# Turned tiles of the MLP's hidden layer: four places of halves, two places for the last tile, and steps begun one pair sooner

## The chip, the cores and the metric

The kernel runs on one core of a Trainium2 chip. The metric is the device time of one execution in microseconds (us). TensorE is called PE, VectorE DVE, ScalarE ACT, GpSimd POOL, and SyncE, which issues most of the DMAs, SP.

## The reference

One layer on 256 rows of 2048 features, in float32: a norm, a mixer of an SSD scan and attention (not touched here), its product with w_out, and then an MLP with the square of a relu:

```python
h = h + rmsnorm(mix, norm_mix_post)
hdn = relu(rmsnorm(h, norm_mlp_pre) @ w_up)      # 256 x 8192
h = h + rmsnorm((hdn * hdn) @ w_down, norm_mlp_post)
```

The change is in the MLP. The 8192 hidden features are made in two halves of 4096, each with its part of w_up and then its part of w_down.

## The kernel before, in words

**Products.** A float32 product is made of three matmuls in a reduced format: each operand is split into a high half `hi` (made by ACT, line 148) and the rest `lo` (made by DVE, line 149), and high x high, high x low and low x high are added up. The weights come as raw blocks of 128 x 2 x 512 (512 KB) through `fetch` (line 162, on SP), and are then split. Where a Strassen-like scheme replaces eight block products by seven (`seven`, lines 423 to 457), DVE also makes sums of blocks (line 263), and one raw block comes in two DMAs (lines 157 and 158), half of it a sum that POOL's DMAs made in memory.

**Units.** `unit` (line 488) makes 2 x 512 columns for both tiles of 128 rows: a list of pairs of row tiles of the contraction, some by seven products and the others as plain row tiles (`row_tiles`, lines 368 to 370). For w_up the pairs are 0 to 6, of which 1, 3, 4 and 6 go by seven, and pair 7 as plain row tiles at the end. After the last pair by seven, `combine_new` (lines 459 to 468) puts the four sums of products together: ACT copies one (line 464), and DVE adds (lines 465 to 468) into four tiles, `room["shared"]`: two in hb and two called wpost. Line 468 is the last and writes `b[1]`, the second wpost tile. After that, pair 7 ends in the other four banks, `up_end` adds them to the tiles (line 1491), and the two sets of four banks change roles. So the next unit's first row tiles want the banks that the combine reads.

**Turned tiles.** Each of a unit's four finished tiles (128 rows x 512 hidden features) has to be turned, since w_down contracts over the features. `turned` does this in two steps, beside the next unit's products:

- first step, begun by `pump_beside`: ACT takes the relu (line 1500) and the square (line 1501), and writes the tile's words as separate 16-bit halves (line 1502) into a place of `room["halves"]`; a transposing DMA on SP (line 1503) turns the halves back into the tile's own memory.
- second step, run by `land_beside` or `drain_beside`: ACT puts the halves together to words again (line 1506) in a tile called junk, of which there is one, and ACT and DVE split it (lines 148 and 149) into sh and sl or ah and al, where w_down reads them.

There are two places of halves (for four tiles). A unit begins the first step of one tile before each of its pairs from the third on (`if i >= 2`), and the second step after more than two further pairs. What is left after the last pair by seven is finished by `drain_beside` ahead of the combine. The order of instructions on each engine is set by a scheduler from priorities; an engine runs its instructions in that order.

**Places of raw weights.** Besides four places of its own pool, the raw weights use memory that is free at the time: in w_up's first half two parts of mw0, all of mw2 and three parts of ha (10 places in all, while mw1 holds the halves); in the second half two parts of ha (6 in all), while the first part of ha holds the halves. The last w_down begins with two parts of uc and what the halves left of ha, and adds the place of the halves (`more_in_place`) once all tiles are turned.

Of the kernel before, what the change touches and what calls it, by code (L numbers as in the profile page):

```python
# [17 lines left out]
P = 128  # L18
# [60 lines left out]
def hymba_layer(ctx: ExitStack, tc: tile.TileContext, x, norm_mix_pre, w_in, conv_w, conv_b, dt_bias, a_log,  # L79
# [113 lines left out]
    def beside_up(raws, turn, halves=None):  # L193

        room["sums"] = [v[:, k:k + KB] for k in range(0, NK // 2, KB) for v in att[1]]
        b = hp.tile([P, NT, NB], F32, name="hb")
        room["shared"] = [[b[:, t] for t in range(NT)],
                          [hp.tile([P, NB], F32, name="wpost", bufs=2) for _ in range(NT)]]
        a = hp.tile([P, 3 * KB, NB], F32, name="ha")
        in_a = [a[:, k:k + KB] for k in range(0, 3 * KB, KB)]  # L200
        halves = in_a.pop(0) if halves is None else halves
        room["halves"] = deque(halves[:, i].bitcast(U16) for i in range(KB))
        room["raw"], room["turn"], room["acts"], room["chain"] = [*raws, *in_a], turn, act_u, True
        room["of_halves"], room["of_a"] = halves, in_a
        sums_of.clear()

    def beside_down():

        a = hp.tile([P, 3 * KB, 2, S], F32R, name="ha")
        room["sums"] = [a[:, k] for k in range(3 * KB)]  # L210
        room["raw"], room["turn"], room["acts"], room["then"] = [mws[2]], 0, part, more_beside_down
        sums_of.clear()

    def more_beside_down():
# [273 lines left out]
    def unit(src, n, order, last, acc, more, combine, lag=0, at_end=(None, None), first=True, ending=None,  # L488
# [3 lines left out]
        cols = blocks_of(n)  # L492
        sevens = [k for k, by_seven in order if by_seven]
        for i, (k, by_seven) in enumerate(order):
            if i >= 2:
                pump_beside()
            if i + 1 < len(order) and order[i + 1][1]:
                sums_of_acts(order[i + 1][0])
            if by_seven:
                if k == sevens[0]:  # L500
                    drain()
                    if ready:
                        ready()
                seven(src, *cols, k, acc, more, k == sevens[0], k == sevens[-1])
            else:
                for b in range(2):
                    row_tiles(src, cols[b], [k], acc[b::2], room["acts"], first and i == 0, False,
                              fetch=fetch_next)
            land_beside()
            if k == sevens[-1]:  # L510
                drain_beside()
                combine(more)
        for b in range(2):
            if b and ending:
# [960 lines left out]
    def out_of_place():  # L1475

        yield from copies(in_dram, of_h, 4)
        beside_up([*tiles_of(mws[0], (0, NB)), mws[2]], -2 * RAWS, mws[1])
        for k in UP_SEVENS:
            sums_of_acts(k)  # L1480
            yield
# [13 lines left out]
    def turned(t, k, r):  # L1495
# [6 lines left out]
        nc.scalar.activation(halves.rearrange("p (h n) -> p h n", h=2), words.rearrange("p (n h) -> p h n", h=2), AF.Copy)  # L1502
        nc.sync.dma_start_transpose(words.rearrange("p (n s) -> p n s", s=P), halves)
        yield
        whole = hp.tile([P, NB], F32, name="junk")
        nc.scalar.activation(whole.bitcast(U16).rearrange("p (n h) -> p h n", h=2), words.rearrange("p (h n) -> p h n", h=2), AF.Copy)  # L1506
        d_h, d_l, i = part(k)
        split(d_h[:, i:i + 4, ts], d_l[:, i:i + 4, ts], whole.rearrange("p (f s) -> p f s", f=4))

    def onto_new_mw(more):  # L1510

# [14 lines left out]
    for hf in range(2):  # L1526
        if hf:
            beside_up([], 0)
        for fb in range(0 if hf else 2, 8, 2):
            unit(w_ups[hf], fb, orders[("up", hf), fb], (7,), acc, more,  # L1530
                 lambda x: combine_new(room["shared"], x), 0, (up_end(fb, 0), up_end(fb + 1, 1)))
            acc, more = more, acc
# [24 lines left out]
    def more_in_place():  # L1557
# [1 line left out]
        b = hp.tile([P, KB, 2, S], F32R, name="hb")  # L1559
        room["sums"] += [b[:, k] for k in range(KB)]  # L1560
        room["turn"] %= RAWS + len(room["raw"])
        room["raw"].append(room["of_halves"])
        for n in range(2):
            load_wpost(norm_mlp_post, n)

    room["then"] = more_in_place
    unit(w_downs[1], 0, orders[("down", 1), 0], (14, 15), acc, more,
         lambda x: combine_onto(0, x), 0, (complete(0), complete(1)))
    room["chain"] = False
# [36 lines left out]
```

## Time and profile before

| | |
|---|---|
| median of 3 runs | 1448.58 us (1446.73 to 1452.11) |
| the profiled execution | 1448.34 us |
| its span, first to last instruction | 1446.6 us |
| PE, DVE, ACT busy | 99%, 90%, 69% of the span |
| mean DMA rate | 235 GB/s |
| L1506, junk<-hb and junk<-wpost | 14 + 14 operations, median 1.37 us each |

A row of the profile names the source line, engine, operation, and tiles as out<-in, with shapes as partitions x elements. In the timeline the first number is the start from the beginning of the span, the second the duration; a bracket gives the idle time of the engine just before, and what ended it. A wait for several semaphores is put down to the one that came last. A line can be that of a helper: all high halves are on L148, all low halves on L149. The w_up units of the second half run from about 1110 to 1273 us, and the last w_down follows.

### The profile page before, as it was taken

What the parts mean: (1) busy time and instruction counts of PE and PEld (TensorE: products, weight loads), DVE (VectorE), ACT (ScalarE), POOL (GpSimd) and SP (SyncE); (2) the same over time, 40 slices, a digit from 0 to 9 for tenths busy, and PEclk for the clock granted to TensorE, in tenths of its full rate; (3) what the DMA queues carried; (4) which work ended last, traced back from release to release, by engine and by line L of the source; (5) the groups of instructions that cost most, each with busy time, mean ns of one, the idle gap of its engine ahead of it and who ended that gap; (6) DMA issues with size and microseconds to landing.
All of it is one profiled execution on the core that took longest, in us unless ns stands there. A gap on an engine that the chain in (4) does not pass through costs nothing. (4 is left out here: it accounts for less than half of the span.)

```text
span 1446.6 us, 20277 instructions
## 1 busy us (share of the span) xinstructions
PE 1432.3 (99%) x6930; PEld 1201.5 (83%) x6930; DVE 1297.6 (90%) x1881; ACT 1000.4 (69%) x1407; POOL 162.6 (11%) x244
## 2 busy tenths in 40 slices
PE   9999999999999999999999999999999999999998
PEld 8888888888888888888888888878888878877886
DVE  7788888988999778689988999999889989989998
ACT  7577669666666666556667668986565689987664
POOL 0201110131111000011100011011111111111000
PEclk9999999999999999999999999999999999999999
DMA  8977656756888648588976799798888999999864
GB/s 268 273 217 225 190 175 186 236 175 195 232 245 255 192 126 251 168 268 261 275 235 213 203 340 288 197 266 244 257 254 262 253 268 288 247 280 293 264 197 150
DMA packets 201927, 340.31 MB, mean 235 GB/s; under 512 B 45616, under 2 KB 48544, under 8 KB 201824
## 3 DMA queue, kind: packets, MB, share of 16 engines
q1 hardware_dynamic: 174304, 279.72, 62.0%
q0 software_dynamic: 19648, 45.63, 15.5%
q10 hardware_dynamic: 7872, 13.68, 2.8%
q8 instruction: 54, 0.88, 0.3%
q14 instruction: 49, 0.40, 0.1%
HBM read 327.39 MB, written 49.84 MB: 261 GB/s over the span
## 5 line engine op out<-in xcount | busy, mean ns | idle before, releaser
L149 DVE TENSOR_TENSOR lo<-raw,hi 128x1024 fp32r<-128x1024 f32 (+1 forms) x390 | 472.6, 1217 | 82.8 <-ACT hi L148 80.6
L148 ACT ACTIVATE hi<-raw 128x1024 fp32r<-128x1024 f32 (+1 forms) x390 | 406.2, 1048 | 170.2 <-PE acc L370 49.1
L526 PE MATMUL acc<-ua,hi 128*128 128x512 f32 x520 | 141.2, 400 | 0.1
L148 ACT ACTIVATE hi<-e 128x1024 fp32r<-128x1024 f32 x66 | 69.7, 1057 | 53.8 <-DVE e L263 50.2
L526 PEld LDWEIGHTS acc<-ua,hi 128*128 128x128 f32 x520 | 91.2, 189 | 14.2 <-ACT hi L148 0.2
L368 PE MATMUL acc<-hi,ua 128*128 128x512 f32 x228 | 90.4, 396 | 0.4 <-DVE wpost L468 0.4
L368 PE MATMUL acc<-hi,sh 128*128 128x512 f32 x220 | 86.6, 394 | 3.0 <-DVE wpost L468 3.0
L369 PE MATMUL acc<-lo,ua 128*128 128x512 f32 x228 | 89.2, 391 | 0.0
L370 PE MATMUL acc<-hi,ua 128*128 128x512 f32 x228 | 89.1, 391 | 0.0
L149 DVE TENSOR_TENSOR lo<-e,hi 128x1024 fp32r<-128x1024 f32 x66 | 80.4, 1218 | 6.4 <-ACT hi L148 6.2
L370 PE MATMUL acc<-hi,sl 128*128 128x512 f32 x220 | 85.7, 390 | 0.0
L369 PE MATMUL acc<-lo,sh 128*128 128x512 f32 x220 | 85.6, 389 | 0.0
L529 PEld LDWEIGHTS acc<-ua,lo 128*128 128x128 f32 x520 | 76.5, 189 | 8.9
L529 PE MATMUL acc<-ua,lo 128*128 128x256 f32 x520 | 78.8, 281 | 0.0
L456 PE MATMUL acc<-lo,ah 128*128 128x512 f32 x180 | 70.6, 392 | 0.7 <-DVE lo L149 0.7
L457 PE MATMUL acc<-hi,al 128*128 128x512 f32 x180 | 70.1, 389 | 0.0
L455 PE MATMUL acc<-hi,ah 128*128 128x512 f32 x180 | 70.1, 389 | 0.0
L526 PE MATMUL acc<-uc,hi 128*128 128x512 f32 x208 | 61.4, 405 | 0.0
L149 DVE TENSOR_TENSOR lo<-ha,hi 128x1024 fp32r<-128x1024 f32 x48 | 58.3, 1218 | 3.0 <-ACT hi L148 2.7
L148 ACT ACTIVATE hi<-ha 128x1024 fp32r<-128x1024 f32 x48 | 50.2, 1050 | 6.9 <-PE acc L370 2.0
L456 PE MATMUL acc<-lo,ua 128*128 128x512 f32 x137 | 53.4, 390 | 0.2 <-DVE lo L149 0.2
L455 PE MATMUL acc<-hi,ua 128*128 128x512 f32 x137 | 53.5, 391 | 0.0
(565 smaller groups left out, 3717.0 us busy)
## 6 DMA issues: line engine op xcount, KB each, us to landing
raw<-in_w_in_dram SPq DMA_DIRECT2D x154, 512.0 KB, 4.4
raw<-in_w_down_dram SPq DMA_DIRECT2D x70, 512.0 KB, 5.7
raw<-in_w_up_dram SPq DMA_DIRECT2D x65, 512.0 KB, 5.0
raw<-in_w_out_dram SPq DMA_DIRECT2D x38, 512.0 KB, 5.2
raw<-pair SPq DMA_DIRECT2D x59, 256.0 KB, 4.7
pair<-in_w_up_dram POOLq DMA_DIRECT2D x56, 256.0 KB, 5.8
pair<-in_w_down_dram POOLq DMA_DIRECT2D x52, 256.0 KB, 5.9
ha<-in_w_up_dram SPq DMA_DIRECT2D x25, 512.0 KB, 6.8
```

The lines of the kernel that those rows point to most:

```text
L148: return (nc.scalar.activation(hi, src, AF.Copy), nc.vector.tensor_tensor(lo, src, hi.bitcast(F32), op=ALU.subtract))
L149: nc.vector.tensor_tensor(lo, src, hi.bitcast(F32), op=ALU.subtract))
L368: nc.tensor.matmul(dst[:, cs], a_h[:, r, ts], hi[:, j, cs], start=begin and j == 0, stop=False)
L369: nc.tensor.matmul(dst[:, cs], a_h[:, r, ts], lo[:, j, cs], start=False, stop=False)
L370: product[t] = nc.tensor.matmul(dst[:, cs], a_l[:, r, ts], hi[:, j, cs], start=False, stop=end and j == KB - 1)
L455: nc.tensor.matmul(dst, a_h, hi[:, j], start=own and first, stop=False)
L456: nc.tensor.matmul(dst, a_h, lo[:, j], start=False, stop=False)
L457: nc.tensor.matmul(dst, a_l, hi[:, j], start=False, stop=own and last)
L526: nc.tensor.matmul(acc[f], hi[:, j, f * P:(f + 1) * P], u(k0 + j), start=k0 + j == 0, stop=False, skip_group_check=True)
L529: nc.tensor.matmul(acc[f][:, 0], lo[:, j, f * P:(f + 1) * P], u(k0 + j)[:, 0], start=False, stop=k0 + j == NK - 1, skip_group_check=True)
```

## The change

- `turned` puts the words together in the tile's own place of halves, not in junk, and splits from there.
- There are four places of halves in place of two: mw1 and one part of mw0 in w_up's first half, two of the three parts of ha in its second. The raw weights have 9 places instead of 10 in the first half, 5 instead of 6 in the second. The last w_down begins with one place fewer, and gets two instead of one when all tiles are turned.
- `b[1]`, the tile turned last, has two places in turn: the wpost tile and the memory of junk.
- In w_up the first steps begin at the unit's second pair (`room["first"]` is 1), in w_down at the third as before. `drain_beside` isn't called in a unit any more: at this pace the last second step follows the last pair by seven.

```diff
@@ beside_up
+        room["last"] = deque([room["shared"][1].pop(), hp.tile([P, NB], F32, name="junk")])
+        room["shared"][1].append(room["last"][0])
         a = hp.tile([P, 3 * KB, NB], F32, name="ha")
         in_a = [a[:, k:k + KB] for k in range(0, 3 * KB, KB)]
-        halves = in_a.pop(0) if halves is None else halves
-        room["halves"] = deque(halves[:, i].bitcast(U16) for i in range(KB))
+        halves = halves or [in_a.pop(0) for _ in range(2)]
+        room["halves"] = deque(v[:, i].bitcast(U16) for v in halves for i in range(KB))
         room["raw"], room["turn"], room["acts"], room["chain"] = [*raws, *in_a], turn, act_u, True
-        room["of_halves"], room["of_a"] = halves, in_a
+        room["of_halves"], room["of_a"], room["first"] = halves, in_a, 1
...
@@ unit
-            if i >= 2:
+            if i >= room.get("first", 0):
                 pump_beside()
...
             land_beside()
             if k == sevens[-1]:
-                drain_beside()
                 combine(more)
...
@@ out_of_place
-        beside_up([*tiles_of(mws[0], (0, NB)), mws[2]], -2 * RAWS, mws[1])
+        some, more_raw = tiles_of(mws[0], (0, NB))
+        beside_up([more_raw, mws[2]], -2 * RAWS, [mws[1], some])
...
@@ turned
-        whole = hp.tile([P, NB], F32, name="junk")
-        nc.scalar.activation(whole.bitcast(U16).rearrange("p (n h) -> p h n", h=2), words.rearrange("p (h n) -> p h n", h=2), AF.Copy)
+        nc.scalar.activation(halves.rearrange("p (n h) -> p h n", h=2), words.rearrange("p (h n) -> p h n", h=2), AF.Copy)
         d_h, d_l, i = part(k)
-        split(d_h[:, i:i + 4, ts], d_l[:, i:i + 4, ts], whole.rearrange("p (f s) -> p f s", f=4))
+        split(d_h[:, i:i + 4, ts], d_l[:, i:i + 4, ts], halves.bitcast(F32).rearrange("p (f s) -> p f s", f=4))
...
@@ the loop over w_up's units
         for fb in range(0 if hf else 2, 8, 2):
+            room["last"].rotate(1)
+            room["shared"][1][1] = room["last"][0]
             unit(w_ups[hf], fb, orders[("up", hf), fb], (7,), acc, more,
...
@@ the last w_down
-        room["raw"].append(room["of_halves"])
+        room["raw"] += room["of_halves"]
...
-    room["then"] = more_in_place
+    room["then"], room["first"] = more_in_place, 2
```

The changed kernel's lines stand two or three further down: the combine's 464 to 468 are 467 to 471 there, 1491 is 1494, and the turning's 1500 to 1503 and 1506 are 1503 to 1506 and 1508.

The first place is DVE at the end of w_up's last unit, where the combine stands. Before, with hb and wpost as the four tiles and al<-junk as the split of a turned tile's rest:

```order
L466 TENSOR_TENSOR hb<-acc,r 128x512
L467 TENSOR_TENSOR wpost<-acc,r 128x512
L1491 TENSOR_TENSOR hb<-acc,hb 128x512
L149 TENSOR_TENSOR lo<-raw,hi 128x1024
L1491 TENSOR_TENSOR hb<-acc,hb 128x512
L149 TENSOR_TENSOR lo<-raw,hi 128x1024 x3
L415 TENSOR_TENSOR r<-r 128x256
L149 TENSOR_TENSOR al_4885<-junk,ah_4884 128x4x128
L149 TENSOR_TENSOR lo<-raw,hi 128x1024
L416 TENSOR_TENSOR r<-r 128x128
L468 TENSOR_TENSOR wpost<-acc,wpost 128x512
```

And in the changed kernel, at the same place:

```order
L468 TENSOR_TENSOR r<-hb,ps 128x512
L149 TENSOR_TENSOR lo<-raw,hi 128x1024
L469 TENSOR_TENSOR hb<-acc,r 128x512
L470 TENSOR_TENSOR wpost<-acc,r 128x512
L1494 TENSOR_TENSOR hb<-acc,hb 128x512
L471 TENSOR_TENSOR wpost<-acc,wpost 128x512
L1494 TENSOR_TENSOR hb<-acc,hb 128x512
L149 TENSOR_TENSOR lo<-raw,hi 128x1024
L1494 TENSOR_TENSOR wpost<-acc,wpost 128x512 x2
```

The combine's last addition has moved from the far side of a turned tile's split and five low halves to the second row after the one before it.

The second place is ACT in the same unit. Before, from the combine's copy (line 464) to the last tile's line 1506:

```order
L464 ACTIVATE hb<-ps 128x512
L148 ACTIVATE hi<-raw 128x1024
L1506 ACTIVATE junk<-wpost 128x2x512
L148 ACTIVATE hi<-raw 128x1024 x2
L148 ACTIVATE ah_4884<-junk 128x4x128
L148 ACTIVATE hi<-raw 128x1024 x2
L1500 ACTIVATE hb<-hb,rmlp 128x512
L1501 ACTIVATE hb<-hb 128x512
L1502 ACTIVATE ha<-hb 128x1024
L148 ACTIVATE hi<-raw 128x1024
L1506 ACTIVATE junk<-wpost 128x2x512
```

In the changed kernel, from the last tile's line 1505 (1502 before) to its split; here its place is junk, and ha holds the halves:

```order
L1505 ACTIVATE ha<-junk 128x1024
L148 ACTIVATE hi<-raw 128x1024
L1508 ACTIVATE ha<-hb 128x2x512
L1508 ACTIVATE ha<-wpost 128x2x512
L148 ACTIVATE hi<-e 128x1024
L148 ACTIVATE hi<-raw 128x1024
L148 ACTIVATE hi<-r 128x512
L148 ACTIVATE ah_4884<-ha 128x4x128 x2
L1508 ACTIVATE ha<-junk 128x2x512
L467 ACTIVATE hb<-ps 128x512
L148 ACTIVATE hi<-raw 128x1024 x3
L148 ACTIVATE ah_4884<-ha 128x4x128
```

The putting together of all four tiles has moved ahead of the combine's copy, from behind it and behind the next unit's first steps.

More of the change, by code (lines that the diff above doesn't have):

```diff
@@ L211, in beside_down @@
         room["raw"], room["turn"], room["acts"], room["then"] = [mws[2]], 0, part, more_beside_down
+        room["first"] = 2
         sums_of.clear()
```

## The prediction

> **What bounds the kernel now.** I read the page first, for the share of each engine.
>
> ```profile
> span 1446.6 us, 20277 instructions
> PE 1432.3 (99%) x6930; PEld 1201.5 (83%) x6930; DVE 1297.6 (90%) x1881; ACT 1000.4 (69%) x1407; POOL 162.6 (11%) x244
> ```
>
> PE is covered almost throughout, so any gain has to come out of places where its matmuls are held up. A matmul's listed duration (0.39 us) overlaps with its neighbours'; the beat is the distance between starts. In the timeline of PE for the first w_up unit, these are the first and the last of 197 matmuls that follow each other undisturbed:
>
> ```profile
> 819.79 0.39 PE L456 MATMUL acc<-lo,ah 128*128 128x512 f32 x1
> ...
> 864.21 0.39 PE L370 MATMUL ps<-hi,ua 128*128 128x512 f32 x1
> ```
>
> 196 distances in 44.42 us are 0.2266 us each. A unit of w_up has 4 pairs by seven products (21 matmuls each) and 4 pairs by row tiles (24 each), 180 matmuls: 40.8 us is its floor. The waits of PE say what holds the beat up, over the whole execution (waited for; us, times, longest):
>
> ```profile
> PE acc L368 <- DVE wpost L468: 3.4, 3, 2.0
> PE ps L369 <- DVE lo L149: 1.2, 2, 0.7
> PE acc L456 <- DVE lo L149: 0.9, 2, 0.7
> ```
>
> The first is the largest of the kernel: the first row tile of the next unit wants an accumulator bank that the last of the combine's additions (L468) hasn't read yet. Its worst case is the start of the last w_down, in PE's timeline:
>
> ```profile
> 1273.18 0.39 PE L369 MATMUL ps<-lo,sh 128*128 128x512 f32 x1
> 1275.55 0.50 PE L368 MATMUL acc<-hi,sh 128*128 128x512 f32 x1 [1.99 <-DVE wpost L468]
> 1275.89 0.39 PE L369 MATMUL acc<-lo,sh 128*128 128x512 f32 x1
> ```
>
> From start to start it loses 2.37 - 0.23 = 2.14 us, and the next start comes 0.11 late as well, since the beat is taken up slowly. Why L468 is late is seen in the timelines of DVE and ACT. Its neighbour L467 ran ten microseconds before it:
>
> ```profile
> 1265.12 0.68 DVE L467 TENSOR_TENSOR wpost<-acc,r 128x512 f32<-128x512 f32 x1
> 1271.79 0.68 DVE L149 TENSOR_TENSOR al<-junk,ah 128x512 fp32r<-128x512 f32 x1
> 1274.81 0.68 DVE L468 TENSOR_TENSOR wpost<-acc,wpost 128x512 f32<-128x512 f32 x1
> ```
>
> ```profile
> 1262.03 1.36 ACT L1506 ACTIVATE junk<-wpost 128x1024 uint16<-128x1024 uint16 x1
> 1273.34 1.33 ACT L1506 ACTIVATE junk<-wpost 128x1024 uint16<-128x1024 uint16 x1
> ```
>
> L468 writes the wpost tile that the second L1506 still reads. That L1506 writes junk, of which there is one, and so comes after the split (al<-junk) of the tile before it. One tile's combine thus stands behind the whole file of turned tiles.
>
> The waits of ACT and DVE from 1150 to 1275 us show what else the file costs:
>
> ```profile
> ACT junk L1506 <- DVE sl L149: 6.7, 2, 3.4
> ACT ha L1502 <- DMA hb<-ha: 2.5, 1, 2.5
> ACT hi L148 <- DMA raw<-in_w_down_dram: 2.1, 3, 1.5
> DVE lo L149 <- ACT hi L148: 7.0, 13, 2.7
> ```
>
> ACT stands twice for junk and once for a place of halves that a transposing DMA still reads, and DVE then stands for ACT's high halves, 7.0 us. The second kind recurs in w_down, on ACT and then on DVE, just ahead of one of PE's waits for lo:
>
> ```profile
> 1293.57 1.06 ACT L1502 ACTIVATE ha<-wpost 128x1024 uint16<-128x1024 uint16 x1 [2.59 <-DMA hb<-ha]
> 1296.82 1.23 DVE L149 TENSOR_TENSOR lo<-e,hi 128x1024 fp32r<-128x1024 f32 x1 [2.48 <-ACT hi L148]
> ```
>
> **The change, part by part.** *Work.* No instruction is added: L1506 still makes one pass over 128x1024 halves, only into its own halves, and the split reads from there. PE's 6930 matmuls stay, so the floor stays. Everything is a matter of waits.
>
> *The combine (gain).* With two places for the last tile, and the steps begun at the unit's second pair, L468 waits for no L1506 and follows L467 by one other DVE operation of the same size, 0.68 us. At 1265.12 that means an end near 1267, 6 us ahead of PE's 1273.18, so the wait goes wholly. In the chain that ended last, the first matmul after a wait stands with more than its followers:
>
> ```profile
> 1275.55 0.50 PE acc L368
> 1276.05 0.23 PE acc L369
> ```
>
> So the three cases are 3.4 us waited plus 3 x 0.27 us of slow take-up. I take -4.2 us. The bounds are 0, if PE then waits for something else, and -4.2.
>
> *Splits that come late (gain).* PE's four waits for lo are 1.2 + 0.9 = 2.1 us, with 4 x 0.27 of take-up 3.2 us. The first and the last of them in PE's timeline:
>
> ```profile
> 1165.87 0.50 PE L456 MATMUL acc<-lo,ah 128*128 128x512 f32 x1 [0.69 <-DVE lo L149]
> ...
> 1314.58 0.50 PE L369 MATMUL ps<-lo,sh 128*128 128x512 f32 x1 [0.71 <-DVE lo L149]
> ```
>
> All four lie where turned tiles are in the file. Four places of halves end the wait of L1502, and the split out of the tile's own halves ends that of L1506 for junk; DVE's lo then comes up to 2.5 us sooner. But lo also waits for other things, so I take half: -1.6 us, with 0 and -3.2 as bounds.
>
> *One place of raw weights fewer (cost).* The halves take a place from the raw weights: 10 become 9 in the first half of w_up, 6 become 5 in the second. A unit fetches 16 blocks in 40.8 us, 2.55 us each, so every fetch there may leave 2.55 us later. One of the tighter ones, SP's issue and ACT's use of it:
>
> ```profile
> 1202.24 0.55 SPq L162 DMA_DIRECT2D raw<-in_w_up_dram  x1
> 1210.94 1.05 ACT L148 ACTIVATE hi<-raw 128x1024 fp32r<-128x1024 f32 x1
> DMA to landing us min/median/max: 2.9/5.5/12.2
> ```
>
> 8.7 us lie between issue and use, 5.5 of them the median way of a w_up block: 3.2 us to spare become 0.65. Before, ACT's list of waits has no w_up block in it. A median block still comes in time; one that takes 8 us comes 1.9 us late on ACT. PE runs on split weights and feels only what outlasts that stock. I take +1.0 us; the bounds are 0 and +9.5, which is 1.9 us once in each of the five units of w_up that have tiles to turn (two in its first half, three in its second).
>
> *The steps, one pair sooner (cost).* The four passes per turned tile (L1500 to L1502, and the transposing DMA on SP) stand ahead of weights that they stood behind; each DMA holds SP's later fetches until ACT has made its halves. They are the same passes and the same number of DMAs, and what is moved ahead is missing behind, at the turn to the next unit. That is a net of 0. But the last tile's way has become short: in ACT's new order (the second place shown above) 8 operations stand between its L1502 and its L1506. Their lengths from start to start are in ACT's timeline, and the way of the transposing DMA in the view of its line:
>
> ```profile
> 1207.31 1.36 ACT L1506 ACTIVATE junk<-hb 128x1024 uint16<-128x1024 uint16 x1
> 1208.54 1.98 ACT L148 ACTIVATE hi<-raw 128x1024 fp32r<-128x1024 f32 x2
> 1210.42 0.62 ACT L148 ACTIVATE sh<-junk 128x512 fp32r<-128x512 f32 x1
> DMA to landing us min/median/max: 2.7/6.8/10.3
> ```
>
> An L1506 takes 1.23 us, a high half of 1024 0.94, one of 512 0.52 (to the 1210.94 above). Two, three and three of them are 6.8 us. Behind that L1506 on ACT are the combine's copy (L464) and the next weights' high halves, and behind those DVE and PE. At the median nothing is lost, at the longest 10.3 - 6.8 = 3.5 us of ACT, in each of the five units: 0 to +17 us of ACT, most of it taken up by the stock of split weights. I take +0.9 us. The Trainium skill's page "DMA: Bandwidth & Descriptors", section "Latency and other measured facts", gives DMA transposes about 261 GB/s. For a tile of 128x1024 halves (262 KB) that is an estimated 1.0 us of transfer; by it this term would be 0 and the sum 0.9 us lower. The 6.8 us of the trace speak against that here, as the sum has it.
>
> *Sum.* -4.2 - 1.6 + 1.0 + 0.9 = -3.9 us. The profiled execution took 1448.34 us, 1.7 more than its span; the median of the three runs is 1448.58. From 1448.5, between the two, -3.9 gives 1444.6 us.
>
> **The rivals.** *DVE is the next bound (no change).* The windows of the three w_up units (us; PE, PEld, DVE, ACT, POOL busy):
>
> ```profile
> 1150.00:1190.00 40.00, 38.94 (x169) 31.29 (x169) 35.44 (x42) 34.02 (x41) 5.04 (x8) 1.00 1.02 274
> 1190.00:1231.00 41.00, 41.00 (x180) 33.32 (x179) 39.94 (x49) 37.41 (x46) 5.28 (x8) 1.00 1.03 280
> 1231.00:1273.00 42.00, 41.97 (x185) 34.39 (x185) 40.51 (x49) 39.60 (x49) 4.08 (x6) 1.00 0.93 244
> ```
>
> In a full unit DVE has about 40 us of work against PE's 40.8. If its order leaves it idle for over 0.8 us per unit, it falls behind, and the 4.2 us come back as waits for lo. For it: DVE was busy 40.51 of 42. Against it: it idled 7.1 of the 123 us, 7.0 of them behind ACT, and the waits that stopped ACT are the ones that go. The price is all of the gain but some 0.5 to 1 us: 1447 to 1449, say 1448. The Trainium skill's page "Perfetto Trace Analysis", section "Identifying the Most-Contended Engine", takes an engine's occupancy as how near VectorE is to its limit and says to work on the fullest engine first. By that rule this change, which takes no work from DVE, would bring nothing; so far the trace bears it out only in that DVE's share is so high.
>
> *The fetches come late (slower).* The place is ACT's high half of a raw block in w_up's second half, with 5 places. It decides if blocks take 8 us rather than 5.5, which the DMA share of 1.02 and 1.03 in these windows makes possible. Then about 5 of 16 blocks in a unit come 1.9 us late; with 0.8 us per unit and the stock to take them up, some 2 us per unit reach PE, in four units +8, less the 4.2 gained: 1452. Against it stands that ACT waits for no w_up block today.
>
> *Every stop of ACT goes and nothing comes back.* Both gains in full and no cost: -4.2 - 3.2 = -7.4, 1441. It takes both new costs at 0, which the margins of 0.65 and 0 us speak against.
>
> *It doesn't do what it says.* If L468 still stood behind a turned tile, nothing would change. DVE's new order (the first place shown above) excludes this: no split stands between L467 and L468.
>
> **How the numbers follow.** The forecast has 0.57, DVE next 0.22, late fetches 0.12, everything gained 0.09. 0.5% (7.2 us) is about what a measurement of this kernel can tell from no change: the three runs before lie 5.4 us apart. The forecast and the first rival lie within it. Faster by more takes under 1441.4: nearly all of the best case's half, 0.06. Slower by more takes over 1455.8: the upper tail of the late fetches, 0.04. The range reaches from 1441.2, just over the best case, to 1449.8, which holds the first rival and leaves out the late fetches' upper part.
>
> **What would show it.** Right: PE's waits have no L468 (now L471) in w_up and at both starts of w_down; ACT's have no wait for junk or halves; L471 ends within 4 us of L470. The combine's term is wrong if PE still waits at 1273. The slot term is wrong if ACT waits for raw or ha of w_up by over 2 us in all, the step term if ACT's L1506 (now L1508) waits for a DMA by over 3 us in all. If the L468 waits are gone and the time is the same, DVE is next, and PE's waits for lo will have grown by about 4 us. A time under 1441 or over 1450 makes the prediction wrong.

## The result, and the profile after

The changed kernel takes 1466.66 us (median; 1464.0 to 1471.46), the kernel before 1449.83 in the same comparison: a ratio of 1.0121, 95% interval 1.0085 to 1.0158. It is slower, by 17 us. The prediction had 1444.6 with a range up to 1449.8, so it has the wrong sign of the change and its range does not hold the time. The profiled execution took 1464.0 us.

The page of the changed kernel, for comparison with the first lines shown of before:

```profile
span 1461.9 us, 20229 instructions
PE 1439.8 (98%) x6930; PEld 1204.5 (82%) x6930; DVE 1297.7 (89%) x1881; ACT 999.6 (68%) x1407; POOL 162.7 (11%) x244
```

The work is the same to a microsecond on DVE and ACT, and PE has its 6930 matmuls. All 15 us of span are waits and what follows on them: PE's waits in the MLP are 12.7 us against 5.5 before, and in about as much again PE counts as busy with the same matmuls (1439.8 against 1432.3 us), in part at half its clock (last section). PE's waits over the whole execution (us in total, times, longest), less those outside the MLP:

```profile
PE acc L458 <- ACT hi L148: 5.8, 2, 3.7
PE ps L372 <- DVE lo L149: 2.7, 4, 0.8
PE ps L371 <- ACT hi L148: 2.2, 1, 2.2
...
PE acc L372 <- DVE lo L149: 1.0, 2, 0.8
PE acc L458 <- ACT mw L148: 0.8, 1, 0.8
...
PE ps L459 <- DVE lo L149: 0.2, 1, 0.2
```

The wait that the change aimed at (for the combine's last addition, L468 before and L471 now) is gone, all three times. In its place stand waits for ACT's high halves, 8.0 us in three places, which the kernel before did not have at all. Starts of equal matmuls in the two traces, subtracted, say where the time went: the forecast gains are there (1.3 us near 942, 1.2 at 1169, 0.7 at 1190, 1.8 at 1276), about 5 us in all, and against them stand losses of about 20 us: 1.1 at 573 to 579 in code that the change doesn't touch, 0.5 at 932, 3.4 in the first w_down (969 to 1011), 5.1 at 1224, 3.2 from 1269 to 1299, and 6.9 at 1321 to 1337. The first varies from run to run: experiment 3, whose engines have the same order there, lacks it. Two of these stops can be read in the timelines.

**The stop at 1224.** ACT, at the end of a w_up unit (start, duration, operation; the bracket is idle time and what ended it):

```profile
1218.88 1.14 ACT L148 ACTIVATE sh<-ha 128x512 fp32r<-128x512 f32 x2
1223.80 1.34 ACT L1508 ACTIVATE ha<-wpost 128x1024 uint16<-128x1024 uint16 x1 [3.78 <-DMA wpost<-ha]
1225.01 1.03 ACT L148 ACTIVATE hi<-raw 128x1024 fp32r<-128x1024 f32 x1
1225.94 0.58 ACT L467 ACTIVATE hb<-acc 128x512 f32<-128x512 f32 x1
```

The transposing DMA it waits for, on SP (the listed duration is that of its issue, not its way to landing):

```profile
1214.30 4.20 SPq L1506 DMA_TRANSPOSE wpost<-ha  x1
```

ACT came to the putting together (L1508) of the tile turned last at about 1220, and stood there until the transposing DMA had landed, 9.5 us after its issue. Behind it stood the high half that PE's next matmuls needed and the combine's copy (L467). PE at the same time:

```profile
1223.47 0.39 PE L460 MATMUL ps<-hi,uc 128*128 128x512 f32 x1
1226.09 0.50 PE L371 MATMUL ps<-hi,uc 128*128 128x512 f32 x1 [2.23 <-ACT hi L148]
1227.35 0.50 PE L372 MATMUL ps<-lo,uc 128*128 128x512 f32 x1 [0.76 <-DVE lo L149]
...
1228.49 0.63 PE L373 MATMUL ps<-hi,uc 128*128 128x512 f32 x1
1228.92 0.63 PE L371 MATMUL ps<-hi,uc 128*128 128x512 f32 x1
```

3.78 us of ACT became 2.23 + 0.76 us of waiting on PE (3.4 us from start to start above the beat), and then the matmuls started 0.43 us apart instead of 0.23 for a while, which makes the 5.1 us.

**The stop at 1327 to 1337.** SP in the last w_down of the changed kernel:

```profile
1308.83 1.23 SPq L1506 DMA_TRANSPOSE wpost<-ha  x1
1324.46 0.37 SPq L162 DMA_DIRECT2D ha<-in_w_down_dram  x1
```

SP issued nothing for over 14 us. Its waits from 1275 to 1345 name the reason, the split of a turned tile's rest (al):

```profile
SPq L162 <- DVE al L149: 10.2, 1, 10.2
...
SPq L162 <- DMA wpost<-ha: 4.1, 1, 4.1
```

Of the 14.4 us, 4.1 went by until the transposing DMA itself had landed, as before; the other 10.2 are the wait for the split. That split, on DVE:

```profile
1323.69 0.69 DVE L149 TENSOR_TENSOR al<-ha,ah 128x512 fp32r<-128x512 f32 x1
```

The fetch writes into a place of halves in ha. Before, such a place was free as soon as the transposing DMA had read it. Now the tile is put together in the same place, and the place is taken until ACT and DVE have split it. The fetch stands at the head of SP's queue, the other fetches behind it, and PE ran out of blocks:

```profile
1329.77 0.50 PE L458 MATMUL acc<-hi,ah 128*128 128x512 f32 x1 [2.12 <-ACT hi L148]
...
1334.23 0.80 PE L458 MATMUL acc<-hi,ua 128*128 128x512 f32 x1 [3.73 <-ACT hi L148]
```

Here too PE's clock was halved, for longer than at 1224 (last section).

### The profile page after: what moved, and what is told of

Read it like the earlier page. It is cut to its first block, busy times and chain, and to the rows that moved or that the text cites. A ratio compares the mean times of both kernels' runs of the same rounds, so it can differ in the third digit from the quotient of the medians.

```text
span 1461.9 us, 20229 instructions
## 1 busy us (share of the span) xinstructions
PE 1439.8 (98%) x6930; PEld 1204.5 (82%) x6930; DVE 1297.7 (89%) x1881; ACT 999.6 (68%) x1407; POOL 162.7 (11%) x244
## 5 line engine op out<-in xcount | busy, mean ns | idle before, releaser
L149 DVE TENSOR_TENSOR lo<-raw,hi 128x1024 fp32r<-128x1024 f32 (+1 forms) x402 | 488.2, 1219 | 88.0 <-ACT hi L148 84.9
L148 ACT ACTIVATE hi<-raw 128x1024 fp32r<-128x1024 f32 (+1 forms) x402 | 418.5, 1049 | 180.5 <-PE acc L373 51.4
L371 PE MATMUL acc<-hi,ua 128*128 128x512 f32 x228 | 90.1, 395 | 0.0
L373 PE MATMUL acc<-hi,ua 128*128 128x512 f32 x228 | 89.0, 390 | 0.0
L149 DVE TENSOR_TENSOR lo<-e,hi 128x1024 fp32r<-128x1024 f32 x66 | 80.5, 1220 | 1.4 <-ACT hi L148 1.4
L458 PE MATMUL acc<-hi,ua 128*128 128x512 f32 x137 | 53.5, 397 | 3.7 <-ACT hi L148 3.7
L460 PE MATMUL acc<-hi,ua 128*128 128x512 f32 x137 | 53.3, 389 | 0.0
L149 DVE TENSOR_TENSOR lo<-ha,hi 128x1024 fp32r<-128x1024 f32 x40 | 48.7, 1221 | 4.8 <-ACT hi L148 4.6
```

Of the source, the lines that this page charges most:

```text
L148: return (nc.scalar.activation(hi, src, AF.Copy), nc.vector.tensor_tensor(lo, src, hi.bitcast(F32), op=ALU.subtract))
L149: nc.vector.tensor_tensor(lo, src, hi.bitcast(F32), op=ALU.subtract))
L371: nc.tensor.matmul(dst[:, cs], a_h[:, r, ts], hi[:, j, cs], start=begin and j == 0, stop=False)
L373: product[t] = nc.tensor.matmul(dst[:, cs], a_l[:, r, ts], hi[:, j, cs], start=False, stop=end and j == KB - 1)
L458: nc.tensor.matmul(dst, a_h, hi[:, j], start=own and first, stop=False)
L460: nc.tensor.matmul(dst, a_l, hi[:, j], start=False, stop=own and last)
```

## The experiments

The theories, by their letters in the expectations:

- Q: the steps begun a pair sooner hold SP's fetches back, or leave the tile turned last too short a way.
- P: the one place of raw weights fewer is the cause.
- H: in the last w_down the fetch into a place of halves waits for the last split.
- L: a place of halves that is put together in itself stays taken until its split, and so holds what is queued behind it.
- O: the single junk had an effect of its own. Each tile had to wait for the split of the one before, which kept the turned tiles apart in ACT's order. Without it the scheduler packs them closely, and the last one comes before its transposing DMA has landed.

Each ratio is against the kernel before, run on the same chip in the same comparison; the interval is of 95%.

### 1. The steps as before, all else changed

```diff
-        room["of_halves"], room["of_a"], room["first"] = halves, in_a, 1
+        room["of_halves"], room["of_a"], room["first"] = halves, in_a, 2
             if k == sevens[-1]:
+                drain_beside()
                 combine(more)
```

> The changed kernel with its steps put back: begun at a w_up unit's third pair, the rest finished ahead of the combine. Four places of halves and the two places for the last tile stay. Theory Q (transposing DMAs begun a pair sooner hold SP's later weight fetches, and the last tile's halves are wanted 7 us after they are sent): the stop of ACT near 1220 us (3.8 us) and the 13.2 us of SP near 842 go, and 5 to 9 us of the 17 come back: 1457 to 1461. Theory P (the lost raw places are the cause): no difference, 1464 to 1468.

Measured: 1476.24 us, ratio 1.0178 (1.0149 to 1.0207). Slower still, by 10 us, which neither theory expected. The sooner steps are thus no cause of the loss; with four places put together in themselves they even save something. The largest wait of SP for ACT in w_up and w_down is that of a transposing DMA at the head of its queue (13.2 us in the changed kernel):

```profile
SPq L1507 <- ACT mw L1506: 23.2, 1, 23.2
```

### 2. The steps sooner, and nothing else

Only the kernel before, with the steps at the unit's second pair in w_up (at the third in w_down), and no `drain_beside`:

```diff
-        room["of_halves"], room["of_a"] = halves, in_a
+        room["of_halves"], room["of_a"], room["first"] = halves, in_a, 1
...
-            if i >= 2:
+            if i >= room.get("first", 0):
-                drain_beside()
                 combine(more)
...
-    room["then"] = more_in_place
+    room["then"], room["first"] = more_in_place, 2
```

> The kernel before with nothing but the steps begun a pair sooner in w_up (and no finishing ahead of the combine); two places of halves, junk, one place for the last tile, all raw places. Theory Q: slower than before by 4 to 9 us, 1453 to 1458, with SP's waits for ACT at the transposing DMAs grown. Theory P: no cost, or faster by up to 3 us, since L468's wait shortens.

Measured: 1443.47 us (1442.3 to 1446.15), ratio 0.9957 (0.9944 to 0.9970). It is faster than both kernels, by 6.3 us of the kernel before's 1449.8. PE's waits from 800 to 1345 us, which is all of the turning:

```profile
PE acc L369 <- DVE wpost L469: 1.2, 1, 1.2
PE ps L370 <- DVE lo L149: 1.2, 2, 0.7
PE acc L457 <- DVE lo L149: 0.2, 1, 0.2
```

The three waits of 3.4 us for the combine's last addition (now L469) have become one of 1.2. Theory Q had expected a loss, and P at most 3 us of gain. One part of the change brings its whole gain, and the other parts (four places of halves, two last places) lose 23 us from there. From here on the question is which of them.

### 3. The places of halves given to the fetches later

```diff
-        room["turn"] %= RAWS + len(room["raw"])
-        room["raw"] += room["of_halves"]
+        room["then"] = more_places
...
+    def more_places():
+        n = room["turn"] % (RAWS + len(room["raw"]))
+        if n < RAWS:
+            room["turn"] = n
+            room["raw"] += room["of_halves"]
+        else:
+            room["then"] = more_places
```

> The changed kernel, but the last w_down takes up the two places of halves for raw weights only at its next turn of the places, so that the next fetches go to the pool's own places. Theory H (in the last w_down a fetch into a place of halves waits 10 us on SP for the last turned tile's split, and all later fetches stand behind it): PE's waits near 1327 and 1330 us (2.1 and 3.7 us, with slow matmuls behind them) go: 6 to 8 us less than the changed kernel, 1458 to 1461. Theory P: the places are short there in any case; within 2 us of the changed kernel.

Measured: 1465.33 us, ratio 1.0106 (1.0075 to 1.0137), no gain over the changed kernel that can be told. The fetch no longer met the place of halves, but then the fetches had too few places, and one waited 13.2 us for a low half of weights. PE's stop moved to a later point, 1347 to 1358, and was of about the same size:

```profile
PE acc L371 <- ACT hi L148: 6.3, 1, 6.3
```

This could not tell H from a mere lack of places; experiment 10 does.

### 4. Both edits, 1 and 3

> Both edits: steps back and the places of halves taken up later. If Q and H hold and add up: 1448 to 1454, near the kernel before, with no wait of PE for the combine's last addition. If the lost raw places cost by themselves (P): over 1458.

Measured: 1479.48 us, ratio 1.0207 (1.0177 to 1.0237), as experiment 1 or worse, and far above what Q and H together had expected.

### 5. The steps sooner, with one place of raw weights fewer

Experiment 2 with 9 and 5 places; the idle block is given back where the changed kernel gives it.

```diff
-        beside_up([*tiles_of(mws[0], (0, NB)), mws[2]], -2 * RAWS, mws[1])
+        beside_up([tiles_of(mws[0], (0, NB))[1], mws[2]], -2 * RAWS, mws[1])
...
+        idle = [] if halves else [in_a.pop(0)]
...
+        room["of_halves"], room["of_a"], room["first"] = [*idle, halves], in_a, 1
```

> The kernel before with the steps begun sooner (it measured 1443.5 us) and with nothing else but one place of raw weights fewer: 9 in w_up's first half, 5 in its second; the block left idle is given back once all tiles are turned, as the changed kernel does. Two places of halves, the words put together in junk, one last place. Theory P (the missing places are the cause): the fetches of w_up and of the first w_down leave late, ACT waits for raw blocks by over 10 us, and the time is that of the changed kernel, 1460 to 1468 us. Theory L (a place of halves that is put together in itself stays taken until its split, and so holds what is queued behind it): this has no such place, 1442 to 1448 us. The prediction's own price for the places was 1.0 us with 9.5 as its bound, 1444 to 1453.

Measured: 1447.0 us, ratio 0.999 (0.9981 to 1.0). The place costs 3.5 us against experiment 2, so P alone does not make the loss. By the starts of equal matmuls it lies in the main at one point, 1270 to 1278, where PE waits 3.5 us for the combine's last addition (1.2 in experiment 2) and then runs for 3.4 us at half its clock. The changed kernel has no such wait, so what the place costs there isn't shown.

### 6. Four places of halves, but put together in junk

The changed kernel with junk and one last place, as before.

```diff
+        whole = hp.tile([P, NB], F32, name="junk")
-        nc.scalar.activation(halves.rearrange("p (n h) -> p h n", h=2), words.rearrange("p (h n) -> p h n", h=2), AF.Copy)
+        nc.scalar.activation(whole.bitcast(U16).rearrange("p (n h) -> p h n", h=2), words.rearrange("p (h n) -> p h n", h=2), AF.Copy)
...
-            room["last"].rotate(1)
-            room["shared"][1][1] = room["last"][0]
```

> The changed kernel with the words put together in junk again and with one last place: four places of halves, 9 and 5 raw places, steps sooner. A place of halves is free again when the transposing DMA has read it. P: as slow as the changed kernel, 1460 to 1468 us. L: the loss is gone but for the waits for junk, 1442 to 1450 us.

Measured: 1452.79 us, ratio 1.0024 (1.0013 to 1.0035). It lies 2.8 us above what L had expected. It is 5.8 us slower than experiment 5, from which it differs in nothing but four places of halves for two, and it is 14 us faster than the changed kernel. What more places do is seen on SP, in w_up's first half. Experiment 5, with two places, issues the transposing DMAs of a unit's second, third and fourth tile at

```profile
864.11 3.23 SPq L1504 DMA_TRANSPOSE hb<-mw  x1
...
868.64 2.65 SPq L1504 DMA_TRANSPOSE wpost<-mw  x1
...
876.77 1.23 SPq L1504 DMA_TRANSPOSE wpost<-mw  x1
```

and experiment 6, with four, at

```profile
882.24 1.25 SPq L1504 DMA_TRANSPOSE hb<-mw  x1
...
884.47 4.68 SPq L1504 DMA_TRANSPOSE wpost<-mw  x2
```

although the halves were made at the same times. In experiment 6, on ACT:

```profile
861.62 1.04 ACT L1503 ACTIVATE mw<-hb 128x1024 uint16<-128x1024 uint16 x1
...
867.26 1.04 ACT L1503 ACTIVATE mw<-wpost 128x1024 uint16<-128x1024 uint16 x1
...
875.38 1.04 ACT L1503 ACTIVATE mw<-wpost 128x1024 uint16<-128x1024 uint16 x1
```

The DMAs go out 20, 16 and 11 us after their halves. With two places the fourth tile's halves can't be written before the second tile's transposing DMA has read its own, so that DMA has to come early in SP's order. With four nothing demands it, and it stood behind fetches that wait for places of their own. The first tile's transposing DMA, on the other hand, stood too early: up to 853.47 it held SP, and behind it seven DMAs of weights that go ahead of it in experiment 5. That is the longest wait of SP from 825 to 900 us; in experiment 5 no transposing DMA waited there for more than 3.5 us:

```profile
SPq L1504 <- ACT mw L1503: 15.6, 1, 15.6
```

The changed kernel has the same order, with 13.2 us at the head and delays of 19.5, 16.2 and 10.6 us.

The late DMAs are not all of the 5.8 us. By the starts of equal matmuls in the traces of 5 and 6, 1.9 us are lost at 897 to 904, behind them, but 2.9 at 942 and 1.3 at 1270 to 1285, where PE waits for the combine's last two additions (800 to 1345 us; in experiment 5 one such wait of 3.5):

```profile
PE acc L369 <- DVE wpost L469: 4.1, 1, 4.1
PE acc L369 <- DVE wpost L468: 2.9, 2, 2.6
```

At 942 no DMA was late. The tile that the addition writes had landed at 914.46, and its putting together stood 28 us behind in ACT's order:

```profile
942.45 1.33 ACT L1507 ACTIVATE junk<-wpost 128x1024 uint16<-128x1024 uint16 x1
```

So four places cost 5.8 us beside the one junk, by two changes of order, on SP and on ACT; the second does not show in the changed kernel, whose waits for the combine are gone.

### 7. The changed kernel with one last place

```diff
-            room["last"].rotate(1)
-            room["shared"][1][1] = room["last"][0]
```

> The changed kernel with one place for the tile turned last instead of two in turn; all else as changed. By P and by L alike the second place is not the cause: 1462 to 1470 us. If the two places are a part of the loss (the last tile's passes come ahead of the combine without a wait, and so sooner on ACT), it is faster than the changed kernel by over 3 us.

Measured: 1464.23 us, ratio 1.0116 (1.0085 to 1.0147), the changed kernel's time. The second last place is no cause. It differs from experiment 6 only in putting the words together in the place of halves instead of in junk: that costs 11.4 us. The stops near 1224 and 1330 come back with it (6.1 us at 1228 to 1237 and 8.6 at 1335 to 1346 against experiment 6, in a profiled execution that is the slowest of four). At the first, the tile's putting together came 9.1 us after its landing in experiment 6; here ACT stood 3.81 us for the landing.

### 8. Three places of halves, all places of raw weights

```diff
-        halves = halves or [in_a.pop(0) for _ in range(2)]
-        room["halves"] = deque(v[:, i].bitcast(U16) for v in halves for i in range(KB))
+        halves = in_a.pop(0) if halves is None else halves
+        room["halves"] = deque([*(halves[:, i].bitcast(U16) for i in range(KB)), third.bitcast(U16)])
```

`third` is the memory of junk; one last place.

> The changed kernel with three places of halves, mw1's two (or ha's) and the memory of junk, each tile put together in its own; all raw places kept, 10 and 6; one last place. P: nothing is missing, so the gains stand without the loss, 1440 to 1445 us. L: a place is taken until its split and there are only three, so the first step of a unit's fourth tile waits for the first one's split, ACT and SP stop, 1450 to 1465 us.

Measured: 1460.0 us, ratio 1.0078 (1.0053 to 1.0103). All 10 and 6 places are there, no transposing DMA in w_up is more than about 2 us late, and still the time is 16.5 us above that of experiment 2. So the putting together in the place of halves makes most of the loss without a missing place and without late DMAs in w_up, here with three places for it: by the starts of equal matmuls 4.2 us at 1223 to 1229 and 6.7 at 1327 to 1335. The wait of the fetch in the last w_down is there too, and longer:

```profile
SPq L162 <- DVE al L149: 19.0, 1, 19.0
```

### 9. The last tile's second step in the next unit

```diff
-            land_beside()
+            if k != sevens[-1] or "last" not in room or src is w_downs[1]:
+                land_beside()
             if k == sevens[-1]:
                 combine(more)
```

> The changed kernel, with the second step of the tile turned last in the next unit's first pair in place of ahead of the combine (its two places allow it): on ACT its putting together now stands behind the combine's copy, 3 to 4 operations further from its halves. Theory O (without the wait for junk the scheduler packs the turned tiles' passes so closely that the last one comes before its transposing DMA has landed, and ACT stands there ahead of the combine's copy and the next weights): ACT's wait at 1223.80, 3.8 us, shrinks below 1 us, the stop of PE at 1226 (5.1 us) goes, and the time is 4 to 8 us below the changed kernel's 1466, 1458 to 1462 us. If the missing places of raw weights make that stop: unchanged, 1464 to 1468 us.

Measured: 1460.71 us (1459.88 to 1461.64), ratio 1.0073 (1.0056 to 1.0091): 6.0 us below the changed kernel's 1466.7, though the intervals of the two ratios still touch. On ACT the combine's copy now goes first, and the putting together (now L1509) finds its DMA landed:

```profile
1221.96 0.58 ACT L467 ACTIVATE hb<-acc 128x512 f32<-128x512 f32 x1
...
1227.18 1.36 ACT L1509 ACTIVATE ha<-wpost 128x1024 uint16<-128x1024 uint16 x1
```

By the starts of equal matmuls the stop at 1224 is gone with its whole 5.14 us. That is O: ACT's standing there made the stop, and with junk (experiment 6) the same tile stood far behind its landing.

### 10. Junk for the four tiles turned in the last w_down

```diff
+        if hf and k >= 24:
+            halves = hp.tile([P, NB], F32, name="junk").bitcast(U16)
         nc.scalar.activation(halves.rearrange("p (n h) -> p h n", h=2), words.rearrange("p (h n) -> p h n", h=2), AF.Copy)
```

> The changed kernel, with the four tiles that are turned in the last w_down put together in junk again (free by then), so that their places of halves are free when the transposing DMA has read them. Theory H (the first fetch into a place of halves waits for the last tile's split, 10.2 us at SP's head, and holds the fetches behind it): that wait goes, ACT no longer waits for blocks of w_down at 1320 to 1336, the stop of PE there (6.9 us) goes, 1457 to 1461 us. If the last w_down just has too few places: unchanged, 1464 to 1468 us.

Measured: 1457.03 us (1454.95 to 1459.29), ratio 1.0046 (1.0030 to 1.0062): 9.6 us gained by the medians (7.0 between the two profiled executions; the changed kernel's is the fastest of its four). SP in the last w_down, to hold against the same two rows of the changed kernel:

```profile
1309.23 1.97 SPq L1506 DMA_TRANSPOSE wpost<-ha  x1
1316.42 0.37 SPq L162 DMA_DIRECT2D ha<-in_w_down_dram  x1
```

The fetch goes out 7 us after the last transposing DMA's issue, as soon as that has landed, not 15. SP's waits have no al any more, and of PE's waits from 1275 to 1345 this is left:

```profile
PE ps L372 <- DVE lo L149: 1.4, 2, 0.8
```

By the starts of equal matmuls 6.8 us of the 6.9 are gone at this place. The number of places at that time is the changed kernel's, so it is H and not a lack of places.

### 11. Both edits, 9 and 10

> The two edits before together. O and H: the losses add up, so the gains do too: 1450 to 1456 us, with what is left in w_up's first half and the first w_down. If the one stop only hides the other, no more than the better of the two.

Measured: 1456.68 us (1451.81 to 1460.62), ratio 1.0044 (1.0028 to 1.0059). The two gains do not add up: 10.0 us instead of 15.6, no more than experiment 10 alone. By the starts of matmuls both stops of the second half are gone (5.1 and 5.3 us), but w_up's first half and the first w_down have lost 7.2 us more than in the changed kernel between 579 and 971 us, in a profiled execution (1460.6 us) that is the slowest of ten. There the transposing DMAs are still up to 21 us late on SP. Of the 7.2, 4.8 lie at 898 to 906, where every engine still has the changed kernel's order, behind ACT's standing for the third tile's late DMA. First the changed kernel, then this one:

```profile
894.43 1.37 ACT L1508 ACTIVATE mw<-wpost 128x1024 uint16<-128x1024 uint16 x1 [0.49 <-DMA wpost<-mw]
```

```profile
898.58 1.34 ACT L1511 ACTIVATE mw<-wpost 128x1024 uint16<-128x1024 uint16 x1 [3.50 <-DMA wpost<-mw]
```

Experiment 9 shows 3.0 us of this loss at the same place, and experiment 3, with the changed kernel's order on all engines up to 1308 us, 2.8. So it is not edit 9's: it is what the late DMAs can cost, and it varies from run to run. A further 2.7 us lie at 954 to 966, where experiment 10 shows 1.8 with the changed kernel's order.

### 12. As 11, and w_up's first half as in experiment 2

```diff
-        some, more_raw = tiles_of(mws[0], (0, NB))
-        beside_up([more_raw, mws[2]], -2 * RAWS, [mws[1], some])
+        beside_up([*tiles_of(mws[0], (0, NB)), mws[2]], -2 * RAWS, [mws[1]])
...
-        if hf and k >= 24:
+        if not hf or k >= 24:
...
+            if hf:
                 room["last"].rotate(1)
                 room["shared"][1][1] = room["last"][0]
```

There are two last places in the second half alone.

> The two edits together, and w_up's first half and the first w_down as in the kernel with the steps sooner alone: two places of halves, junk, one last place, 10 places of raw weights. With four places nothing makes a transposing DMA on SP come before the next tile's halves, and in w_up's first half three of them went out 11 to 20 us after their halves. If that, the closely packed passes and the last fetch's wait are all that the change lost, this is within 3 us of the kernel with the steps sooner alone (1443.5), 1442 to 1447 us; the one place fewer in the second half may cost up to 3 of them. If it is over 1450, something else in the second half is still open.

Measured: 1450.25 us, ratio 1.0005 (0.9993 to 1.0017): 16 us of the changed kernel's loss are gone. It misses the upper end of the expectation, 1447, by 3 us. PE's waits from 800 to 1345:

```profile
PE acc L460 <- DVE lo L149: 2.7, 1, 2.7
PE ps L372 <- ACT hi L148: 1.9, 1, 1.9
PE ps L373 <- DVE lo L149: 0.8, 1, 0.8
```

Against experiment 2 nothing is lost up to 1270 us; 4.9 us are lost at 1285 and a net 2.1 more by 1325, in the last w_down, which begins with one place fewer. The rest of 6.8 us is thus placed, but its cause is open: experiment 5 priced a place fewer at 3.5 us, at another point.

## Why the prediction was wrong, point by point

**The distance from landing to putting together** is the quantity that the prediction should have followed for each tile. It is the start of L1506 (L1508, L1509 and so on) on ACT less the landing of the tile's transposing DMA, here for the tile turned last in each of the seven units that have tiles (us):

| kernel | w_up, first half | first w_down | w_up, second half | last w_down |
|---|---|---|---|---|
| before | 3.6, 11.9 | 11.0 | 7.4, 5.1, 10.2 | 2.3 |
| 2: steps sooner alone | 11.1, 4.5 | 10.7 | 11.1, 5.4, 16.0 | 1.8 |
| changed | 0.2, 0.4 | 2.9 | 0.8, 0.0, 0.0 | 4.1 |
| 9: last step in the next unit | 0.6, 5.5 | 2.9 | 8.9, 3.5, 6.2 | 2.4 |

Zero means that ACT stood and waited. With junk there are microseconds to spare nearly everywhere; without it the last tile of four units out of five in w_up comes within half a microsecond of its landing or waits for it.

- **The combine (-4.2 us) and the late splits (-1.6).** The combine's waits went as forecast, all 3.4 us. The late splits did not: PE's waits for lo grew in the changed kernel, from 2.1 to 3.9 us. Experiment 2 measured -6.3 us where the two terms make -5.8, but that is in part luck: in its trace 3.9 us are gained at four of the forecast places, of 4.9 in all, and one wait of 1.2 us for the combine is left. It also shows that the sooner steps alone bring the gain, which the prediction gave to the two last places, the four places and the own putting together as well.
- **One place of raw weights fewer (+1.0, at most +9.5).** Too small, with the right bound, where it could be priced: 3.5 us in experiment 5. The mechanism named was not the one that showed: in the changed kernel ACT waited for w_up's blocks 1.6 us in all, against 1.1 before, and experiment 5 lost its 3.5 us at the combine's last addition.
- **The steps a pair sooner, "a net of 0".** Right of the steps themselves. It failed for the DMAs on SP: the prediction looked at ACT's and DVE's new order and not at SP's. The delay of the transposing DMAs comes from the four places (experiment 6 against 5), which free SP's order from the rule that kept them early. What the delay costs the changed kernel varies: little at 898 in its own trace, 2.8 us more in that of experiment 3.
- **The last tile's way (+0.9, 0 to 17 us of ACT).** This is a step that failed in size. Mechanism and place were right, 8 operations between its halves and its putting together against a transposing DMA of 2.7 to 10.3 us. Moving that step back brought 6.0 us (experiment 9). The sentence that went wrong is that most of it is taken up by the stock of split weights: at 1224 the stock took up next to nothing, and 3.78 us of ACT became 5.1 of PE. The prediction's own sign for this, over 3 us of waiting of L1508 for a DMA, came true: 3.8 at that place, 6.2 in all. The Trainium skill's 261 GB/s of DMA transposes (its page "DMA: Bandwidth & Descriptors", section "Latency and other measured facts"), from which 1.0 us was estimated for a tile, differs from the rows here: the one at 1224 took 9.5 us from issue to landing.
- **What the sum left out.** That a place of halves stays taken until the split stood in the prediction ("the split reads from there") without a price. It is the step that failed most, a cost put at nothing, and the dearest item: 9.6 us by experiment 10, for the last w_down's tiles alone, 6.8 of them seen at the stop itself. The prediction counted when a place is needed, and not when it is given back to the fetches that use the same memory next.
- **The rivals.** DVE did not become the bound: PE's waits for lo are 3.9 us, those for ACT's hi and mw 8.8. PE's waits for lo grew by 1.8 us and not by the 4 that this rival had as its sign. The late fetches had the right sign, but their place was w_up's second half and their cause the missing place; the fetches that came late were in the last w_down, for the split.

Taken together from experiment 2 (1443.5 us) to the changed kernel (1466.7): a place fewer 3.5 (5 against 2), four places 5.8 (6 against 5), put together in the place of halves 11.4 (7 against 6), and the second last place no difference that these runs can tell (1464.2 and 1466.7, with intervals of their ratios that overlap). Each price holds for the order in which the parts were added here. The first two show in good part as waits for the combine's last additions, which the changed kernel does not have, so they are not its shares of the loss; the two stops of the second half, 5.1 and 6.9 us, are read in its own trace, and experiments 9 and 10 remove them. Of the other losses in its trace, those in w_up's first half and the first w_down are gone in experiment 12, which does not tell by which of its edits; the 3.2 us from 1269 to 1299 are not assigned.

## What to carry to other kernels

A wait that is removed may have been what kept an order good: ask what a scheduler will do with the freedom, on the DMA queue as well as on the engines, and follow for each transfer the distance from its landing to its first use. A buffer that serves two steps instead of one is given back later, so its price is read from whoever takes the memory next. Test the parts of a change apart; here one part was worth 6 us and the others lost 23.

## What the runs showed of the hardware that was not expected

After the stop at 1224 PE did not return to its beat at once. The granted clock in windows of the changed kernel (us from, to and length; PE, PEld, DVE, ACT and POOL busy; then the clock, the DMA share and GB/s):

```profile
1224.00:1228.00 4.00, 1.15 (x4) 0.75 (x5) 1.93 (x3) 4.00 (x5) 0.00 (x0) 1.00 0.83 246
1228.00:1230.00 2.00, 2.00 (x7) 1.57 (x6) 2.00 (x3) 2.00 (x4) 0.00 (x0) 0.56 0.81 245
1230.00:1232.00 2.00, 2.00 (x6) 1.56 (x6) 2.00 (x4) 0.83 (x1) 0.55 (x1) 0.59 0.78 218
1232.00:1236.00 4.00, 4.00 (x19) 3.27 (x18) 4.00 (x6) 2.42 (x3) 0.74 (x1) 1.00 0.73 229
```

For a little over 3 us, from about 1228.2 to 1231.6, the clock was near half, and matmuls started 0.43 us apart. Seven of them lost about 0.2 us each, 1.4 of the 5.1 us. The stop before it was 2.62 us from start to start, with one matmul and another of 1.26 us after it; the stop of 2.37 us in the kernel before, at 1273, was followed by the full beat. The second stop had it too, for 6.8 us, through 3.6 of which PE waited:

```profile
1330.60:1337.40 6.80, 3.17 (x8) 2.49 (x9) 5.06 (x6) 4.05 (x5) 0.81 (x1) 0.50 1.03 389
```

The Trainium skill's page "TensorE: Matmul & The Clock Gate", section "Part 1: The HAM clock gate (the "warmup" mystery)", says that the clock is at half after an idle window of about 3.4 us, and that the windows run freely. The lengths of the slow stretches agree with one and two such windows: in all these traces they are 3.41 or 6.83 us, but for the one at the end of the work. The traces also show that PE need not stand for that long: a stop of 1.63 us (start to start) with one of 1.26 right behind it was enough in experiment 8, at 1223, while a single one of 3.0 us in experiment 6, at 942, was not; every single stop of 3.1 us or more in these MLPs had a slow stretch behind or in it. The kernel before and experiment 2 have none ahead of their end. So a stop of PE can cost more than its waits, here 5.1 us for waits of 3.0, which the prediction's 0.27 us of take-up did not have.
